# Column blocks in pairs, two of eight K-tile pairs as seven products of sums, feed-forward in three parts

## The chip, the cores and the metric

The kernel runs on one core of one Trainium2 chip. The metric is device microseconds (us) of one execution, lower is better. A measured time is the median of several executions.

## The reference, cut to what matters

The reference is a two-layer decoder trunk on x of 256 tokens by 2048, all in float32. Layer 0 mixes with a gated unit and sparse attention between two projections, layer 1 with a short convolution between two projections; each layer ends in a feed-forward, and a norm closes the trunk.

```python
def swiglu(h, w_gate, w_up, w_down):
    return (jax.nn.silu(h @ w_gate) * (h @ w_up)) @ w_down      # 2048 -> 5632 -> 2048
...
for i in range(DEPTH):
    hn = rmsnorm(h, norm_mix[i])
    mix = sgu_nsa_mixer(hn, w_in_ab[j], w_out_ab[j], ...) if i % 2 == 0 else short_conv_mixer(hn, w_in_c[j], conv_w[j], w_out_c[j])
    h = h + mix
    h = h + swiglu(rmsnorm(h, norm_ffn[i]), w_gate[i], w_up[i], w_down[i])
return rmsnorm(h, norm_f)
```

## The kernel before, in words

Tokens are two tiles of 128 (m = 0, 1). Every projection is a product of activations (stationary, 128 x 128 tiles) and weights (moving, 128 rows by 512 columns, NW). Both are kept as a sum of two float32r parts, high and low, and a product is three matmuls into one PSUM bank: xh*wh, xh*wl, xl*wh (L99, L100, L101 in `Stream.multiply`).

`Stream` holds the whole order of the work. `gemm` (L44) lays down the units of one column block of 512: a unit is two K tiles, for both m, so 2 x 2 x 3 = 12 matmuls; 2048 rows of weights are 8 units. A block uses two PSUM banks of the pool `pg` (four banks), so blocks alternate. Weights come by SP's queue in loads of 1 MB (two units) into three raw buffers (`load`, L67). `split` (L75) makes a unit's parts: ACT copies the raw tile to `wh` (L82), DVE subtracts it from the raw tile to give `wl` (L83), both 1024 wide. There are four buffers of parts, so splits run three units ahead of PE (`ahead`, L103): the split for unit i+3 is issued behind unit i's matmuls and waits for the buffer of unit i-1. `run` (L111) goes through the units: matmuls, splits ahead, the block's `done` if it was its last unit, then the hooks that were laid on this unit (`at`, `after`). Each engine has its instructions in this order and takes them in order.

In the feed-forward (L746) gate and up blocks alternate, 11 of each per layer; `done_gate_ff` (L760) applies silu on ACT out of PSUM, `done_up` multiplies on DVE out of PSUM (L769), and one unit later eight PE transposes (L227) bring the product to K-major form, which ACT and DVE split (L238, L239). All 44 K tiles of it are kept, and the down projection runs as four column blocks over 44 K tiles, 22 units each. `norm_from` (L268) adds a block's two banks to h (L276), sums squares on ACT (L250), and transposes h for the next operand. The convolution (L792 to L848) has 12 input blocks (cg, z, bg for each of four) and four output blocks. `last` (L865) ends the kernel: the last four units run m by m, so that the first half is normed and stored while the second is multiplied.

At the start SP issues row0, x's first piece (256 tokens by 256 columns), the first raw load, x's second piece, the second raw load, x's third piece, the third raw load; ACT issues the other five pieces of x. The first four raw loads are 512 KB. PE transposes the first two pieces before the first unit.

Of the kernel before, what the change touches and what calls it, by code (L numbers as in the profile page):

```python
# [27 lines left out]
NEG = -1e30  # L28
AHEAD = 3
PROBS, VALUES = 4, 6  # L30


class Stream:


    def __init__(self, nc, raws, parts, psg):
        self.nc, self.raws, self.parts, self.psg = nc, raws, parts, psg
        self.raw_plan, self.units = [], []
        self.raw, self.hl = {}, {}
        self.loaded = self.split_to = 0  # L40
        self.hooks = {}
        self.at_unit = 0

    def gemm(self, w, groups, n0, src, done, tail=0, between=None):  # L44
# [3 lines left out]
        for gi, g in enumerate(groups):  # L48
            k0, gk = g if isinstance(g, tuple) else (g, 4)
            ri = len(self.raw_plan)  # L50
            self.raw_plan.append((w[k0 * P:(k0 + gk) * P, n0:n0 + NW].rearrange("(k p) n -> p k n", p=P), gk * NW))
            for j in range(gk // 2):
                self.units.append({
                    "raw": ri, "j": j, "k0": k0 + 2 * j, "src": src, "chunk": chunk, "free": j == gk // 2 - 1,
                    "first": gi == 0 and j == 0, "last": gi == len(groups) - 1 and j == gk // 2 - 1, "tail": 0,
                })
            if between and gi < len(groups) - 1:
                ap, use = between.pop(0)
                self.units.append({"raw": len(self.raw_plan), "j": 0, "use": use, "free": True})
                self.raw_plan.append((ap, 2 * NW))  # L60
        if tail:
            self.units[-tail]["tail"] = tail

# [3 lines left out]
    def load(self):  # L67
        if self.loaded < len(self.raw_plan):
            ap, n = self.raw_plan[self.loaded]
            t = self.raws.tile([P, 4 * NW], F32, name="raw")  # L70
            self.nc.sync.dma_start(out=t[:, :n].rearrange("p (k n) -> p k n", n=ap.shape[-1]), in_=ap)
            self.raw[self.loaded] = t.rearrange("p (k n) -> p k n", n=NW)
            self.loaded += 1

    def split(self, pieces=(slice(0, 2),)):  # L75
        u = self.units[self.split_to]
        nc = self.nc
        src = self.raw[u["raw"]][:, 2 * u["j"]:2 * u["j"] + 2, :]
        hv = self.parts.tile([P, 2, NW], F32R, name="wh")
        lv = self.parts.tile([P, 2, NW], F32R, name="wl")  # L80
        for ks in pieces:
# [889 lines left out]
```

## Time and profile before

| | us |
|---|---|
| median of three runs | 2187.59 (2186.87 to 2188.07) |
| the profiled execution | 2187.05 |
| its span, first to last instruction | 2185.3 |
| PE busy | 2174.6, 9900 matmuls |
| DVE busy | 1149.6, 1269 instructions |
| ACT busy | 988.3, 1178 instructions |

The span is what the trace covers; the rest of the execution's time lies around it. Busy is the time in which an engine has an instruction running, PE's ends being modelled. In a row of a group, "x767" is a count, the figure before the comma its busy us, the one behind it the mean ns of one instruction.

### The profile page before, as it was taken

The numbers are of one execution on the slowest core, as the hardware profiler recorded it, in microseconds if no ns is written. First come the engines' busy times: TensorE is split into PE (matmuls) and PEld (weight loads), VectorE is DVE, ScalarE is ACT, GpSimd is POOL, SyncE is SP. The second block draws the span as 40 slices with busy tenths as digits, with TensorE's granted clock in tenths as the row PEclk, the third lists the DMA queues.
The fourth block names the chain that finished last, engine by engine and source line by source line (L and its number), as shares of the span: only waits on it lengthen the run. The fifth ranks groups of instructions, "written<-read, shape, count | busy, mean of one in ns | idle before, by whom it ended". The sixth has DMA issues, their size and how long they took to land.

```text
span 2185.3 us, 24414 instructions
## 1 busy us (share of the span) xinstructions
PE 2174.6 (100%) x9900; PEld 1796.8 (82%) x9900; DVE 1149.6 (53%) x1269; ACT 988.3 (45%) x1178; POOL 28.3 (1%) x59
## 2 busy tenths in 40 slices
PE   9999999999999999999999999999999999999998
PEld 7887788888888888888888888888888888888886
DVE  6577655555444544544455555554554455444444
ACT  6456545444444444444444444444444444444443
POOL 2000000000000000000000000000000000000000
PEclk9999999999999999999999999999999999999999
DMA  7664455665555555555556555556555555556553
GB/s 261 204 198 134 136 176 190 193 193 183 188 190 191 192 191 188 188 187 190 192 184 201 185 182 191 190 187 192 192 193 191 188 186 186 192 193 197 197 193 135
DMA packets 214577, 410.95 MB, mean 188 GB/s; under 512 B 6744, under 2 KB 18448, under 8 KB 214464
## 3 DMA queue, kind: packets, MB, share of 16 engines
q1 hardware_dynamic: 210416, 404.52, 56.9%
q10 hardware_dynamic: 3664, 3.63, 0.5%
q8 instruction: 77, 1.26, 0.2%
q0 software_dynamic: 384, 1.25, 0.2%
q14 instruction: 36, 0.29, 0.0%
HBM read 407.27 MB, written 2.10 MB: 187 GB/s over the span
## 4 chain that ended last, share of the span: by engine, by line
PE 99%; issue 0%; DMA 0%; DVE 0%; SPq 0%; POOLq 0%; POOL 0%; ACT 0%; DVEq 0%
PE pg L99 32%; PE pg L101 32%; PE pg L100 32%; PE pm L227 2%; PE pm L537 0%; PE pm L614 0%; PE pm L403 0%; PE pm L570 0%; DMA h<-in_x_dram 0%; PE pm L501 0%; PE pm L688 0%; PE pm L617 0%; PE pm L577 0%; POOLq L966 0%; POOL nf_r L899 0%
## 5 line engine op out<-in xcount | busy, mean ns | idle before, releaser
L83 DVE TENSOR_TENSOR wl<-raw,wh 128x1024 fp32r<-128x1024 f32 (+1 forms) x769 | 939.1, 1224 | 923.0 <-ACT wh L82 920.4
L82 ACT ACTIVATE wh<-raw 128x1024 fp32r<-128x1024 f32 (+1 forms) x769 | 812.0, 1059 | 962.3 <-PE pg L101 952.7
L99 PE MATMUL pg<-wh,a_h 128*128 128x512 f32 x2080 | 820.6, 394 | 0.0
L101 PE MATMUL pg<-wh,a_l 128*128 128x512 f32 x2080 | 810.6, 390 | 0.0
L100 PE MATMUL pg<-wl,a_h 128*128 128x512 f32 x2080 | 810.0, 389 | 0.0
L101 PEld LDWEIGHTS pg<-wh,a_l 128*128 128x128 f32 x2080 | 390.7, 188 | 82.1
L100 PEld LDWEIGHTS pg<-wl,a_h 128*128 128x128 f32 x2080 | 391.0, 188 | 81.7 <-issue 2.2
L99 PEld LDWEIGHTS pg<-wh,a_h 128*128 128x128 f32 x2080 | 390.9, 188 | 81.4 <-issue 2.1
L99 PE MATMUL pg<-wh,t_h 128*128 128x512 f32 x704 | 274.3, 390 | 0.0
L101 PE MATMUL pg<-wh,t_l 128*128 128x512 f32 x704 | 273.9, 389 | 0.0
L100 PE MATMUL pg<-wl,t_h 128*128 128x512 f32 x704 | 273.9, 389 | 0.0
L101 PEld LDWEIGHTS pg<-wh,t_l 128*128 128x128 f32 x704 | 132.1, 188 | 27.4
L100 PEld LDWEIGHTS pg<-wl,t_h 128*128 128x128 f32 x704 | 132.2, 188 | 27.3
L99 PEld LDWEIGHTS pg<-wh,t_h 128*128 128x128 f32 x704 | 132.2, 188 | 27.3
L99 PE MATMUL pg<-wh,y 128*128 128x512 f32 x128 | 50.4, 394 | 0.0
L99 PE MATMUL pg<-wh,z_h 128*128 128x512 f32 x128 | 50.2, 392 | 0.0
L101 PE MATMUL pg<-wh,y 128*128 128x512 f32 x128 | 49.9, 390 | 0.0
L101 PE MATMUL pg<-wh,z_l 128*128 128x512 f32 x128 | 49.9, 390 | 0.0
L100 PE MATMUL pg<-wl,y 128*128 128x512 f32 x128 | 49.8, 389 | 0.0
L100 PE MATMUL pg<-wl,z_h 128*128 128x512 f32 x128 | 49.8, 389 | 0.0
L239 DVE TENSOR_TENSOR t_l<-pm,t_h 128x512 fp32r<-128x512 f32 x44 | 28.4, 686 | 32.4 <-ACT t_h L238 32.4
L238 ACT ACTIVATE t_h<-pm 128x512 fp32r<-128x512 f32 x44 | 23.9, 595 | 46.2 <-PE pm L227 46.2
(182 smaller groups left out, 780.3 us busy)
## 6 DMA issues: line engine op xcount, KB each, us to landing
raw<-in_w_gate_dram SPq DMA_DIRECT2D x88, 1024.0 KB, 5.2
raw<-in_w_up_dram SPq DMA_DIRECT2D x88, 1024.0 KB, 5.2
raw<-in_w_down_dram SPq DMA_DIRECT2D x88, 1024.0 KB, 5.1
raw<-in_w_in_c_dram SPq DMA_DIRECT2D x48, 1024.0 KB, 5.1
raw<-in_w_in_ab_dram SPq DMA_DIRECT2D x34, 1024.0 KB, 5.2
raw<-in_w_out_ab_dram SPq DMA_DIRECT2D x16, 1024.0 KB, 5.1
raw<-in_w_out_c_dram SPq DMA_DIRECT2D x16, 1024.0 KB, 5.1
raw<-in_w_in_ab_dram SPq DMA_DIRECT2D x4, 512.0 KB, 6.7
```

The costliest lines, as they stand in the source:

```text
L82: nc.scalar.activation(hv[:, ks], src[:, ks], AF.Copy)
L83: nc.vector.tensor_sub(lv[:, ks], src[:, ks], hv[:, ks].bitcast(F32))
L99: nc.tensor.matmul(ps[m], xh[:, kt, sl], hv[:, k, :], start=u["first"] and k == 0, stop=False)
L100: nc.tensor.matmul(ps[m], xh[:, kt, sl], lv[:, k, :], start=False, stop=False)
L101: nc.tensor.matmul(ps[m], xl[:, kt, sl], hv[:, k, :], start=False, stop=u["last"] and k == 1)
L227: nc.tensor.transpose(t[:, k * S + m * P:k * S + (m + 1) * P], src[:, m, c + k * P:c + (k + 1) * P], ident)
L238: nc.scalar.activation(dh[:, k0:k0 + 2, :], t, AF.Copy)
L239: nc.vector.tensor_sub(dl[:, k0:k0 + 2, :], t, dh[:, k0:k0 + 2, :].bitcast(F32))
```

## The change

Stages from the first feed-forward on run as blocks of two column blocks (`Stream.block`), n = 0 and 1, over eight pairs of K tiles. A block uses four `pg` banks, one for each n and m (`BANK`). Pairs of K tiles 0 to 3, 5 and 7 are multiplied as before: two units ("n" in the pattern) of 12 matmuls. Pairs 4 and 6 (`SUMS`) go as seven products instead of eight: four units ("s") with 2, 2, 2 and 1 products of three matmuls, some of sums of weights and some of sums of activations. Four of the seven products gather over both pairs in banks P1, P5, P6, P7 of the other pool, which transposes also use; the rest add to the block's own banks. The sums of weights are four DVE additions, 512 wide, ahead of the first "s" unit's split (`sums13`); `sum2` overwrites half of a raw tile. An "s" unit's split is 1024 wide, the fourth's 512. The sums of activations are made when the operand is split (`x_split`): three DVE subtractions and a second split, one unit later.

Behind the unit of the last P5 and P7 products, `summed` puts the four banks together in two SBUF tiles g and u: a copy on ACT, four DVE instructions. When the block ends, `done` adds the block's own banks: n = 0 behind the last unit, n = 1 behind the first unit of the next block. Gate and up are now the two column blocks of one block; silu and product run on SBUF tiles, and their transposes come in two fours at the end of the next block's units 2 and 3. In down and output blocks `add_to_h` adds g and u to h and then the banks to h.

The feed-forward runs in three parts of 4, 4 and 3 gate/up blocks (`PARTS`), each followed by the down product over its own K tiles, two blocks each, added to h. Blocks over 12 K tiles have the order N6 with one pair of seven products. F8 is N8 with the sums one unit later; it is used where an operand is new: each layer's first gate/up block, the first convolution block, the first output block. The last two column blocks of layer 1's last part stay single, as the tail was.

Raw loads are all 512 KB, in six buffers, and eight from the first output block of layer 0 on (`widen`), where the buffers of parts become five, so splits run four units ahead. At the start two raw loads are issued where one was.

```diff
+RAWS = 6
+MORE = 2
...
+PARTS = (4, 4, 3)
+SUMS = {4: 0, 6: 1}
+BANK = ((1, 3), (2, 7))
+P1, P5, P6, P7 = FREE = (0, 4, 5, 6)
...
+    def widen(self, pool):
+        self.ring.insert(self.slot, (pool, len(self.ring)))
+        self.sums = pool
+        self.free += [pool] * MORE
...
+    def block(self, ws, form, src, begun, summed, done):
...
+        for kp, seven in order:
+            k0 = 2 * kp
+            wk = [w[(kb + k0) * P:(kb + k0 + 2) * P, n0:n0 + NW].rearrange("(k p) n -> p k n", p=P) for w, kb, n0 in ws]
+            def t(k, m, k0=k0):
+                return lambda: src.tile(k0 + k, m)
+            def s(i, kp=kp):
+                return lambda: src.sum(kp, i)
+            if not seven:
+                for n in range(2):
+                    queue["n"].append((wk[n], {"frees": 1, "mms": [(k, t(k, m), BANK[n][m]) for m in range(MT)
+                                                                    for k in range(2)]}))
+            else:
+                queue["s"].append((wk, t, s))
+                queue["s"].extend([None] * 3)
...
+                def sums13(ra=ra, rb=rb, ts=ts, sum2=sum2, sum4=sum4):
+                    a, b = self.raw[ra], self.raw[rb]
+                    ts.append(self.sums.tile([P, 3, NW], F32, name="ts", bufs=2))
+                    self.nc.vector.tensor_add(ts[0][:, 0], a[:, 0], b[:, 0])
+                    self.nc.vector.tensor_add(ts[0][:, 1], b[:, 0], b[:, 1])
+                    sum2()
+                    sum4()
...
+                sevens = [
+                    {"raw": ra, "prep": sums13, "frees": 1, "mms": [(0, t(0, 0), P1), (1, t(1, 0), BANK[0][0])]},
+                    {"raw": rb, "frees": 1, "mms": [(0, s(2), P6), (1, s(3), BANK[1][0])]},
+                    {"raw": rb, "ts": ts, "at": 0, "mms": [(0, s(1), P5), (1, s(0), P7)]},
+                    {"raw": rb, "ts": ts, "at": 2, "w": 1, "mms": [(0, t(1, 1), BANK[0][1])]},
+                ]
+                u = sevens.pop(0)
+            else:
+                u = sevens.pop(0)
...
+        self.on(last_sum, lambda: summed(0, chunk["banks"]))
+        self.on(last_sum + 1, lambda: summed(1, chunk["banks"]))
+        end = len(self.units)
+        self.soon[end - 1] = lambda: done(0, chunk["banks"])
+        self.soon[end] = lambda: done(1, chunk["banks"])
+        for u, fn in begun:
+            self.on(first + u, fn)
+    def on(self, unit, fn, *args):
+        self.hooks.setdefault(unit, []).append(lambda: fn(*args))
     def at(self, delay, fn):
         self.hooks.setdefault(self.at_unit + delay, []).append(fn)
...
+        while self.free and self.loaded < len(self.raw_plan):
+            ap = self.raw_plan[self.loaded]
+            pool = self.free.pop(0)
+            t = pool.tile([P, 2 * NW], F32, name="raw", bufs=RAWS if pool is self.raws else MORE)
+            v = t.rearrange("p (k n) -> p k n", n=NW)
+            self.nc.sync.dma_start(out=t.rearrange("p (k n) -> p k n", n=ap.shape[-1]), in_=ap)
+            self.raw[self.loaded] = v
+            self.home[self.loaded] = pool
...
+    def split(self, pieces=None):
+        i = self.split_to
+        u = self.units[i]
...
+            u["prep"]()
+        w = u.get("w", 2)
+        src = u["ts"][0][:, u["at"]:u["at"] + w] if "ts" in u else self.raw[u["raw"]]
+        pool, k = self.ring[self.slot]
+        self.slot = (self.slot + 1) % len(self.ring)
+        hv = pool.tile([P, 2, NW], F32R, name=f"wh{k}")
+        lv = pool.tile([P, 2, NW], F32R, name=f"wl{k}")
+        for ks in pieces or (slice(0, w),):
             nc.scalar.activation(hv[:, ks], src[:, ks], AF.Copy)
+            if "then" in u:
+                u["then"]()
...
-        self.hl[self.split_to] = (hv, lv)
...
+            self.free.append(self.home[u["raw"]])
+        self.load()
...
+        while self.split_to < min(len(self.units), i + 1 + min(len(self.ring) - 1, 2 + i // 8)):
...
+            if i in self.soon:
+                self.soon[i]()
...
+    def x_split(src, dst, kp, gain=None):
+        ks = slice(2 * kp, 2 * kp + 2)
+        if kp not in SUMS:
+            split_T([src.rearrange("p (k m) c -> p k (m c)", k=2)], (dst.h, dst.l), 2 * kp, gain)
+            return
...
+        v = a.rearrange("p (k m) c -> p k (m c)", k=2)
+        nc.vector.tensor_sub(xs[:, 4:6], a[:, 0:2], a[:, 1:4:2])
+        nc.vector.tensor_sub(xs[:, 6], a[:, 0], xs[:, 5])
+        nc.vector.tensor_sub(xs[:, 7], a[:, 2], xs[:, 6])
+        def parts():
+            i = SUMS[kp]
+            nc.scalar.activation(dst.h[:, ks], v, AF.Copy)
+            nc.scalar.activation(dst.sh[:, i], xs[:, 4:], AF.Copy)
+            nc.vector.tensor_sub(dst.l[:, ks], v, dst.h[:, ks].bitcast(F32))
+            nc.vector.tensor_sub(dst.sl[:, i], xs[:, 4:], dst.sh[:, i].bitcast(F32))
+        st.at(1, parts)
+    def x_pair(src, c, dst, kp, gain=None):
+        t = transposed_bank(src, c).rearrange("p k (m c) -> p (k m) c", m=MT)
+        st.at(1, lambda: x_split(t, dst, kp, gain))
...
+    def summed(part, b):
+        if part == 0:
+            g, u = (late["pool"].tile([P, MT, NW], F32, name=n) for n in ("ga", "ub"))
+            late["g"], late["u"] = g, u
+            nc.scalar.activation(g[:, 0], b[P1], AF.Copy)
+            return
+        g, u = late["g"], late["u"]
+        nc.vector.tensor_sub(u[:, 0], b[P6], g[:, 0])
+        nc.vector.tensor_sub(g[:, 1], b[P7], u[:, 0])
+        nc.vector.tensor_sub(u[:, 1], b[P5], g[:, 1])
+        nc.vector.tensor_add(u[:, 0], b[P5], u[:, 0])
...
+    def add_to_h(n2, squares=None):
+        c0 = 2 * n2 * NW
+        def sums(part, b):
+            summed(part, b)
+            if part:
+                for n, t in enumerate((late["g"], late["u"])):
+                    hs = h[:, :, c0 + n * NW:c0 + (n + 1) * NW]
+                    nc.vector.tensor_add(hs, hs, t)
+        def done(n, b):
+            for m in range(MT):
+                hs = h[:, m, c0 + n * NW:c0 + (n + 1) * NW]
+                nc.vector.tensor_add(hs, b[BANK[n][m]], hs)
+            if squares:
+                st.at(1, lambda: [squares(2 * n2 + n, m) for m in range(MT)])
+        return sums, done
     stage = ExitStack()
...
+    N8 = [(k, k in SUMS) for k in range(8)], "nnnnn sns sns sns sns nnn"
+    F8 = [(k, k in (4, 6)) for k in range(8)], "nnnnnn sns sns sns sns nn"
+    N6 = [(k, k in SUMS) for k in range(6)], "nnn nn sn sn sn s nn"
...
+    def feed_forward(layer, rname, norm):
+        c0 = 0
+        for part, nb in enumerate(PARTS):
+            for c in range(c0, c0 + nb):
+                def done(n, b, c=c, kb=4 * c0):
+                    g, u = late["g"], late["u"]
+                    for m in range(MT):
+                        t = (g, u)[n][:, m]
+                        nc.vector.tensor_add(t, b[BANK[n][m]], t)
+                    def later():
+                        for m in range(MT):
+                            r = R[rname][:, m:m + 1]
+                            if n == 0:
...
+                            else:
+                                nc.vector.scalar_tensor_tensor(g[:, m], u[:, m], r, g[:, m], op0=ALU.mult, op1=ALU.mult)
+                    st.at(1, later)
+                def pairs(b, c=c, c0=c0):
+                    if c == c0 and b == 0:
+                        second_operand()
+                    x_pair(late["g"], b * S, src_x, 2 * (c - c0) + b)
+                st.block([(w_gate[layer], 0, c * NW), (w_up[layer], 0, c * NW)], F8 if c == 0 else N8, src_a, begun[:],
+                         summed, done)
+                begun[:] = [(2, lambda p=pairs: p(0)), (3, lambda p=pairs: p(1))]
+            last = part == len(PARTS) - 1
+            for n2 in range(2):
+                if last and layer == 1 and n2 == 1:
+                    break
+                sums, done = add_to_h(n2, norm[0] if last else None)
+                ws = [(w_down[layer], 4 * c0, 2 * n2 * NW), (w_down[layer], 4 * c0, (2 * n2 + 1) * NW)]
+                st.block(ws, N8 if nb == 4 else N6, src_x, begun[:], sums, done)
+                begun[:] = norm[1](n2) if last else []
+            c0 += nb
...
+    squares, pair, scale = norm_from("c1", g_mix[1])
+    feed_forward(0, "f0", (squares, then_pairs(pair, scale)))
...
+        def gated(n, b):
+            if c == 0 and n == 0 and b == 0:
+                second_operand()
+            y = cv[c + n][:, 2 * b:2 * b + 2]
+            t = transposed_bank((late["g"], late["u"])[n], b * S)
+            def later():
+                nc.vector.tensor_mul(y, t, y)
+                st.at(1, lambda: x_split(y.rearrange("p k (m c) -> p (k m) c", m=MT), src_x, 2 * (c + n) + b))
+            st.at(1, later)
+        if c == 0:
+            return done, [(2, lambda: gated(0, 0)), (2, lambda: gated(0, 1)), (3, lambda: gated(1, 0)),
+                          (3, lambda: gated(1, 1))]
+        return done, [(2, lambda: gated(0, 0)), (3, lambda: gated(0, 1)), (4, lambda: gated(1, 0)),
...
+    order = F8
+    for c in (0, 2):
+        for cc in (c, c + 1):
+            done, then = done_cz(cc)
+            st.block([(wc, 0, D + cc * NW), (wc, 0, 2 * D + cc * NW)], order, src_a, begun[:], summed, done)
+            begun[:] = then
+            order = N8
+        done, then = done_bg(c)
+        st.block([(wc, 0, c * NW), (wc, 0, (c + 1) * NW)], N8, src_a, begun[:], summed, done)
+        begun[:] = then
+    squares, pair, scale = norm_from("f1", g_ffn[1])
+    begin = then_pairs(pair, scale)
+    for n2 in range(2):
+        sums, done = add_to_h(n2, squares)
+        st.block([(w_out_c[0], 0, 2 * n2 * NW), (w_out_c[0], 0, (2 * n2 + 1) * NW)], N8 if n2 else F8, src_x, begun[:], sums,
+                 done)
+        begun[:] = begin(n2)
...
+    u0 = len(st.units)
+    for c in (2, 3):
+        w = w_down[1][4 * sum(PARTS[:2]) * P:]
+        st.gemm(w, [0, 4, 8], c * NW, src_x, last(c), tail=AHEAD + 1 if c == 3 else 0)
...
+    free = st.free
     for b in range(3):
+        st.free = free[:2]
         st.load()
         if b < 2:
             x_load(nc.sync, b + 1)
```

## Rows read from the trace of the kernel before

**Rows 1.** Page: busy time, granted clock by slice, shares of the chain

```profile
PE 2174.6 (100%) x9900; PEld 1796.8 (82%) x9900; DVE 1149.6 (53%) x1269; ACT 988.3 (45%) x1178; POOL 28.3 (1%) x59
...
PEclk9999999999999999999999999999999999999999
...
PE 99%; issue 0%; DMA 0%; DVE 0%; SPq 0%; POOLq 0%; POOL 0%; ACT 0%; DVEq 0%
PE pg L99 32%; PE pg L101 32%; PE pg L100 32%; PE pm L227 2%; PE pm L537 0%; PE pm L614 0%; PE pm L403 0%; PE pm L570 0%; DMA h<-in_x_dram 0%; PE pm L501 0%; PE pm L688 0%; PE pm L617 0%; PE pm L577 0%; POOLq L966 0%; POOL nf_r L899 0%
```

**Rows 2.** Stretch of feed-forward 0: us, engines' busy us, clock, DMA share, GB/s

```profile
403.00:805.00 402.00, 402.00 (x1816) 333.65 (x1815) 200.64 (x182) 173.57 (x182) 0.00 (x0) 1.00 0.59 189
```

**Rows 3.** Timeline of ACT, five gate units: start us, us, instruction, idle before

```profile
632.46 1.06 ACT L82 ACTIVATE wh<-raw 128x1024 fp32r<-128x1024 f32 x1 [1.66 <-PE pg L101]
...
643.34 1.06 ACT L82 ACTIVATE wh<-raw 128x1024 fp32r<-128x1024 f32 x1 [1.66 <-PE pg L101]
```

**Rows 4.** Page, costliest groups: first matmul of each triple, by operand

```profile
L99 PE MATMUL pg<-wh,a_h 128*128 128x512 f32 x2080 | 820.6, 394 | 0.0
...
L99 PE MATMUL pg<-wh,t_h 128*128 128x512 f32 x704 | 274.3, 390 | 0.0
...
L99 PE MATMUL pg<-wh,y 128*128 128x512 f32 x128 | 50.4, 394 | 0.0
L99 PE MATMUL pg<-wh,z_h 128*128 128x512 f32 x128 | 50.2, 392 | 0.0
```

**Rows 5.** Waits of engines and SP's queue: total us, times, longest

```profile
ACT wh L82 <- PE pg L101: 952.7, 600, 3.1
DVE wl L83 <- ACT wh L82: 920.4, 670, 3.3
...
ACT wh L82 <- DMA raw<-in_w_in_ab_dram: 2.3, 2, 2.0
...
SPq L71 <- DVE wl L83: 1925.7, 380, 11.8
```

**Rows 6.** Groups of DVE by shape: count, busy us, mean ns, idle

```profile
L83 DVE TENSOR_TENSOR wl<-raw,wh 128x1024 fp32r<-128x1024 f32 x767 | 937.6, 1225 | 923.0 <-ACT wh L82 920.4
...
L540 DVE SCALAR_TENSOR_TENSOR s<-dist,pm 128x256 f32<-128x256 f32 x16 | 6.0, 418 | 4.2 <-PE pm L537 4.1
...
L877 DVE TENSOR_TENSOR h<-h,nfg 128x1024 f32<-128x1024 f32 x3 | 3.7, 1218 | 0.0
...
L901 DVE TENSOR_TENSOR h<-h,nfg 128x512 f32<-128x512 f32 x2 | 1.4, 689 | 0.0
```

**Rows 7.** Groups of ACT by shape, columns the same

```profile
L82 ACT ACTIVATE wh<-raw 128x1024 fp32r<-128x1024 f32 x767 | 810.9, 1060 | 962.3 <-PE pg L101 952.7 <-ACT wh L82 3.7 <-DMA raw<-in_w_in_ab_dram 2.3
...
L238 ACT ACTIVATE t_h<-pm 128x512 fp32r<-128x512 f32 x44 | 23.9, 595 | 46.2 <-PE pm L227 46.2
```

**Rows 8.** Timeline of DVE: instructions close behind each other, some merged

```profile
121.16 2.36 DVE L83 TENSOR_TENSOR wl<-raw,wh 128x1024 fp32r<-128x1024 f32 x2 [1.84 <-ACT wh L82]
...
138.19 0.19 DVE L419 TENSOR_TENSOR hq<-hw 128x30 f32<-128x30 f32 x1
138.41 0.18 DVE L420 TENSOR_SCALAR hq<-hq 128x30 f32<-128x30 f32 x1
...
627.20 1.29 DVE L239 TENSOR_TENSOR t_l<-pm,t_h 128x512 fp32r<-128x512 f32 x2 [1.47 <-ACT t_h L238]
```

**Rows 9.** Timeline of PE at the start: x's second piece, first matmuls

```profile
6.78 1.12 PE L227 MATMUL pm<-ident,h 128*128 128x128 f32 x4 [0.31 <-DMA h<-in_x_dram]
...
8.65 0.63 PE L101 MATMUL pg<-wh,a_l 128*128 128x512 f32 x1
9.08 0.63 PE L99 MATMUL pg<-wh,a_h 128*128 128x512 f32 x1
```

**Rows 10.** Stretches at the start, columns as in rows 2

```profile
3.00:7.00 4.00, 3.42 (x15) 2.61 (x14) 0.64 (x3) 1.34 (x4) 3.44 (x16) 1.00 0.99 312
7.00:10.00 3.00, 3.00 (x10) 2.38 (x10) 2.21 (x6) 1.82 (x5) 2.59 (x10) 1.00 1.06 391
```

More of the change, by code (lines that the diff above doesn't have):

```diff
@@ L49, in gemm @@
             k0, gk = g if isinstance(g, tuple) else (g, 4)
[L50 to L56, printed above, removed]
+            for k in range(k0, k0 + gk, 2):
+                ri = self.plan(w[k * P:(k + 2) * P, n0:n0 + NW].rearrange("(k p) n -> p k n", p=P))
+                self.units.append({"raw": ri, "k0": k, "src": src, "chunk": chunk, "frees": 1, "first": gi == 0 and k == k0,
+                                   "last": gi == len(groups) - 1 and k == k0 + gk - 2, "tail": 0})
@@ L91, in multiply @@
         u = self.units[i]
-        ps = u["chunk"]["ps"]
         hv, lv = self.hl[i]
-        xh, xl = u["src"]
+        c = u["chunk"]
+        if "mms" in u:
+            for x, (j, op, key) in enumerate(u["mms"]):
+                uses = c["uses"][key]
+                if uses[0] == (i, x):
+                    c["banks"][key] = self.bank(key)
+                ps = c["banks"][key]
+                xh, xl = op()
+                nc.tensor.matmul(ps, xh, hv[:, j, :], start=uses[0] == (i, x), stop=False)
+                nc.tensor.matmul(ps, xh, lv[:, j, :], start=False, stop=False)
+                nc.tensor.matmul(ps, xl, hv[:, j, :], start=False, stop=uses[-1] == (i, x))
+            return
+        ps = c["ps"]
         for k in range(2):
@@ L849, in done_bg @@
+            for m in range(MT):
+                hs = h[:, m, c * NW:(c + 1) * NW]
+                nc.vector.tensor_add(hs, ps[m], hs)
+                squares(c, m)
+            st.at(1, lambda: pair(2 * c))
+            st.at(1 if c < 3 else 2, lambda: pair(2 * c + 1))
+            if c == 3:
+                st.at(3, scale)
         return done
     for c in range(4):
-        st.gemm(wc, G4, D + c * NW, src_a, done_cg(c))
-        st.gemm(wc, G4, 2 * D + c * NW, src_a, done_z(c))
-        st.gemm(wc, G4, c * NW, src_a, done_bg(c))
@@ new lines, in open_conv, with done_cz, done, conv @@
+    def open_conv():
+        cv["p"] = top.enter_context(tc.tile_pool(name="convt", bufs=2, reuse_waits="tile"))
+        r2 = cv["r2"] = const.tile([P, MT], F32, name="r2")
+        nc.vector.tensor_mul(r2, R["c1"], R["c1"])
+    def done_cz(c):
+        def done(n, b):
+            if c == 0 and n == 0:
+                open_conv()
+            g, u = late["g"], late["u"]
+            for m in range(MT):
+                t = (g, u)[n][:, m]
+                nc.vector.tensor_add(t, b[BANK[n][m]], t)
+            def later():
+                if n:
+                    nc.vector.tensor_mul(g, u, g)
+                else:
+                    for m in range(MT):
+                        nc.scalar.activation(g[:, m], g[:, m], AF.Copy, scale=cv["r2"][:, m:m + 1])
+            st.at(1, later)
+        def conv(b):
+            if b == 0:
+                cv[c] = cv["p"].tile([P, 4, S], F32, name="zc")
+            v = transposed_bank(late["g"], b * S)
+            def later():
+                for k in range(2):
+                    kt = 4 * c + 2 * b + k
+                    o, z = cv[c][:, 2 * b + k], v[:, k]
+                    nc.scalar.activation(o, z, AF.Copy, scale=g_conv[2][:, kt:kt + 1])
+                    for j, lag in ((1, 1), (0, 2)):
+                        nc.vector.scalar_tensor_tensor(o[:, lag:], z[:, :S - lag], g_conv[j][:, kt:kt + 1],
+                                                       o[:, lag:], op0=ALU.mult, op1=ALU.add)
+            st.at(1, later)
+        return done, [(2, lambda: conv(0)), (3, lambda: conv(1))]
```

321 lines of the change are left out of this document (160 added, 161 removed).

## The prediction

> **What bounds the kernel now.** I read the page first. PE is busy for the whole span, the granted clock is full in every slice, and the chain that ended last is 99% PE, nearly all of it the three matmuls of the split product; DVE is busy 53% and ACT 45% [rows 1]. A table by stretch says the same of the feed-forward alone: PE 402.0 of 402.0 us, DVE 200.6, ACT 173.6, DMA 0.59 [rows 2]. So in the stages that change, time is the number of matmuls times their pace. The pace is read from ACT's copies, which follow PE's units of 12 matmuls: from 632.46 to 643.34 us there are four steps, so 2.72 us a unit and 0.2267 us a matmul [rows 3]. (The rows' 390 ns is a latency; the matmuls overlap.) The page's groups count 2080+704+128+128 = 3040 such triples, 9120 matmuls [rows 4], or 2067 us.
>
> Nobody feeds PE late: ACT waits 952.7 us for PE to give back a buffer of parts, DVE waits 920.4 us for ACT, and SP's loads wait 1925.7 us for DVE to be done with a raw buffer [rows 5]. All three walk in step behind PE.
>
> The profiled execution took 2187.05 us around a span of 2185.3; the median of the runs is 2187.59, 0.54 more. The sum is made against 2187.05.
>
> **The change, part by part.**
>
> *Fewer matmuls.* A pair of K tiles with a pair of column blocks needs 2x2x2 = 8 products of three matmuls; as seven it needs 21 matmuls in place of 24. I count the pairs in the code. Gate/up: 11 blocks in each of two layers, two pairs each: 44. Down: four N8 blocks a layer (16 pairs in all), two N6 blocks in layer 0 and one in layer 1 (3 pairs); the last two column blocks of layer 1 stay plain. Convolution: 6 input blocks and 2 output blocks, 16 pairs. That is 79 pairs, 237 matmuls, 237 x 0.2267 = **53.7 us** less. Shapes and the number of transposes stay. PE has no wait to win back, so nothing is gained beyond this.
>
> *More vector work.* Per pair, instead of two splits of 1024 wide (1.225 us) there are three and one of 512, and four sums of 512 (0.69 us between SBUF tiles) [rows 6]: 1.92 + 2.76 = 4.7 us, over 79 pairs 369 us. The 41 blocks each assemble four PSUM results, 4 x 0.69 (113 us). Then: two adds of 1024 into h for 13 down/output blocks (1.22 each, 32 us), PSUM adds of gate/up (61), down (22) and convolution (16), and the sums of the activations for 18 operand pairs at about 1.7 us (30; priced by the 256-wide row of 0.42). DVE goes from 1150 to about 1793 us, some 84% of the new span. A gate/up block costs DVE 12 x 1.225 + 2 x (3 x 1.225 + 0.69) + 18 x 0.69 + 2 x 0.69 = 37.2 us against PE's 186 x 0.2267 + 0.9 = 43.1; a down block 36.9 against 42.2. ACT: 1.69 us more a pair (1.06 a full copy, 0.6 a half) [rows 7] and 48 us of copies: about 1170 us, 55%. Both fit beside PE on average.
>
> *The order.* DVE takes its queue in order, so I walk it where a deadline stands. Independent instructions come closer than their length: two of 686 ns in 1.29 us and two of 1225 in 2.36, a pace of 0.60 and 1.13; an instruction that needs the one before starts 0.03 us after its end (0.19 long, 0.22 apart) [rows 8]. ACT's copy puts a split's start 1.09 us after PE returned the buffer.
>
> The first deadline is the accumulator banks. A block uses all four, and the next block's first unit starts with the bank that the first add of `done` must have read. In a gate/up block DVE has, from the end of the last unit of sums, 11.56 us of PE time (units of 2.72, 0.68 and 3 x 2.72): split and assembly until 5.3, three splits until 8.6, and the add only waits for PE: no loss. A down or output block in N8 order adds 2 x 1.13 for h: 1.42 + 1.13 + 2.64 (assembly) + 2.26 + 3 x 1.13 + 0.69 = 11.53 against 11.56, no margin; I take 0.2 us for each of nine, 1.8 (ends 0 and 1.0 each). In N6, and in the one F8 output block, only two units lie behind the sums: 8.84 us of PE time against 1.42 + 1.13 + 2.64 + 2.26 + 2 x 1.13 + 0.69 = 10.4: PE waits 1.6 us, four times, **6.4 us** (ends 0 and 2.4 each).
>
> The second is PE's transposes of gate x up at the end of unit 2. Before them DVE has `done(1)`, a split, the four sums for the first unit of sums, a split and the product: ready 7.4 us after the block's start, needed at 8.16. Margin 0.7, no loss taken (end 0.5 for 22 blocks). After the convolution's gating, `parts` for the pair of tiles 4 comes one unit before its use behind five other instructions: 0.6 us, once.
>
> *Start.* x's second piece now stands behind two raw loads instead of one, 512 KB more. PE starts its transposes when that piece lands (6.78 us) [rows 9], with the DMA engines saturated: 312 GB/s from 3 to 7 us, 391 from 7 to 10 [rows 10], so it comes 1.3 to 1.7 us later. The third piece stands behind 1 MB more, about 3 us, and has a unit of time. I take +1.5, ends 0 and 3 (that piece late as well). The 2.3 us that ACT waited for early raw loads [rows 5] were not on PE's path. Loads are halved in size and doubled in number; six, then eight, buffers of 512 KB keep more in flight than three of 1 MB, and the DMA share rises as the time shrinks, 0.59 to about 0.61. Cost nothing; were the cover gone, PE would wait for raw tiles. SP only issues loads.
>
> *Feed-forward in three parts, the end.* The down products keep their count; only the h adds above are new. The end (add, squares, scale, store) is as before: nothing.
>
> Sum: -53.7 + 1.5 + 6.4 + 1.8 + 0.6 = -43.4; 2187.05 - 43.4 = 2143.65, and with the 0.54 of the runs **2144.2 us**.
>
> **Rivals.**
>
> *Full drain.* If DVE's independent instructions don't overlap in these chains, each costs its length plus 0.03. Then the N8 down deadline is missed by 0.95 us (nine times), N6 and F8 by 2.4 (four), the transposes by 0.15 (22), with start and gating as above: 8.6 + 9.6 + 3.3 + 2.1 = 23.6, about 2157 us. The Trainium skill states just that ("VectorE: DVE Perf Modes", section "The DRAIN you can't avoid"): the next instruction does not issue until the pipeline is empty, and chaining without semaphores gains nothing. The paces of 0.60 and 1.13 in [rows 8] disagree with it for plain sequences; the new chains have more dependences.
>
> *DVE falls behind in the stretches of sums.* The four sums (2.6 us) precede the split of the first unit of sums in a queue that also carries the splits for the next 2.72 us unit. If buffer returns and ACT's copies do not line up, each pair costs PE 0.4 us: 79 x 0.4 = 32 us more, about 2176. Against it: four units of lookahead, some 8 us.
>
> *Slower.* PE's waits at the bank handover cost it its pace. At the start, where PE has had gaps, matmuls come 0.43 us apart (8.65 and 9.08) [rows 9], close to what the lower of the two clock levels, 1.2 GHz, would give, though the granted clock of that stretch is written as 1.00 [rows 10]; later, with PE never idle, they come 0.2267 apart. If a handover waits and the next unit of 12 runs at that pace, it costs 12 x 0.2 = 2.4 us beside a wait of 1.6; at all 41 blocks 164 us, about 2298. It decides for "slower" from 54/41 = 1.3 us a block. The Trainium skill ("TensorE: Matmul & The Clock Gate", section "A second HAM failure mode: psum-queue depth-cycling") describes a clock that falls and rises where PE idles briefly between groups of matmuls as banks are cycled; no row here shows it, as PE does not wait.
>
> That the saving itself is not made is hardly possible: the instruction count fixes it.
>
> **How the numbers follow.** A measurement of this kernel tells about 0.2% (4.4 us) from no change, so faster means under 2183. Forecast with its own bounds, 2136 to 2153: 0.66. Everything hidden, 2133 to 2136: 0.05. Full drain, 2153 to 2166: 0.12. DVE behind: 0.09, of which 0.02 ends within 0.2%. Slower by the clock or by a stall of this size at every block: 0.08. Range 2133 to 2166 (0.83). Faster 0.90, same 0.02, slower 0.08.
>
> **What would show it.** PE's count 9900 less 237, PE busy near 100% outside the start, clock full in every slice; DVE near 84%, ACT near 55%; small PE waits for the `h` adds at the ends of N6 blocks and none elsewhere; x's second piece landing near 8.3 us. It would be wrong if PE shows waits for splits (`wl`) inside blocks, if DVE's pace in the sums is over 0.72 us, if the clock falls in any slice, or if SP's loads are waited for.

## The result, and the profile after

The changed kernel took 2151.99 us (median of 4 runs, 2151.69 to 2152.04) beside 2187.38 for the kernel before on the same chip: ratio 0.9838, 95% interval 0.9821 to 0.9855. That is 35.4 us less. Forecast were 43.4 less and 2144.2 us; the time lies in the range, the direction is right, and 7.8 us of cost were not in the sum. The profiled execution's span is 2149.6 us, 35.7 below the 2185.3 of before.

From the page of the changed kernel: busy time by engine, granted clock by slice, and the chain by engine and line.

```profile
PE 2128.9 (99%) x9663; PEld 1750.0 (81%) x9663; DVE 1709.6 (80%) x2139; ACT 1145.3 (53%) x1411; POOL 24.1 (1%) x59
...
PEclk9999999999999999999999999999999999999999
...
PE 93%; DVE 3%; issue 2%; ACT 1%; DMA 0%; SPq 0%; POOLq 0%; POOL 0%; DVEq 0%; ACTq 0%
```

Beside [rows 1]: PE has exactly 237 instructions less, it is still the bound, and the clock is full in every slice. DVE has gone from 53% to 80%. The chain now has 7% outside PE.

The waits of PE in the changed kernel: what waited for what, total us, times, longest.

```profile
PE pg L230 <- DVE h L509: 4.8, 3, 1.6
PE pm L371 <- DMA h<-in_x_dram: 1.8, 1, 1.8
PE pg L239 <- DVE h L509: 1.6, 1, 1.6
...
PE pg L240 <- DVE wl L211: 0.8, 1, 0.8
PE pg L239 <- ACT wh L208: 0.7, 1, 0.7
```

The first and third lines are the handover of the accumulator banks, four times. The other lines shown are the first 17 us. No unit inside a block of sevens waits for the split of its weights.

DVE's groups by shape in the changed kernel: count, busy us, mean ns, idle before.

```profile
L211 DVE TENSOR_TENSOR wl<-raw,wh 128x1024 fp32r<-128x1024 f32 x767 | 924.4, 1221 | 253.8 <-ACT wh L208 245.1
...
L138 DVE TENSOR_TENSOR ts<-raw 128x512 f32<-128x512 f32 x79 | 54.7, 692 | 2.7
...
L474 DVE TENSOR_TENSOR ga<-pm,ub 128x512 f32<-128x512 f32 x41 | 28.4, 692 | 4.3
...
L504 DVE TENSOR_TENSOR h<-h,ub 128x1024 f32<-128x1024 f32 x13 | 15.8, 1218 | 0.0
```

Each price is within 4 ns of the one read from [rows 6]. The counts 79, 41 and 13 are those of the forecast.

**The handover as it came.** DVE's timeline at the end of the first N6 block: start us, us, instruction, idle before.

```profile
1030.99 1.23 DVE L211 TENSOR_TENSOR wl<-raw,wh 128x1024 fp32r<-128x1024 f32 x1 [0.21 <-ACT wh L208]
1032.14 0.68 DVE L473 TENSOR_TENSOR ub<-pm,ga 128x512 f32<-128x512 f32 x1
...
1034.86 1.22 DVE L504 TENSOR_TENSOR h<-h,ga 128x1024 f32<-128x1024 f32 x1
1035.99 1.22 DVE L504 TENSOR_TENSOR h<-h,ub 128x1024 f32<-128x1024 f32 x1
1037.12 2.35 DVE L211 TENSOR_TENSOR wl<-raw,wh 128x1024 fp32r<-128x1024 f32 x2
1039.39 1.28 DVE L509 TENSOR_TENSOR h<-pg,h 128x512 f32<-128x512 f32 x2
```

PE's timeline at the same place, and the stretch around it (us, busy us of PE, PEld, DVE, ACT, POOL, clock, DMA share, GB/s).

```profile
1038.24 0.39 PE L232 MATMUL pg<-wh,y 128*128 128x512 f32 x1
1040.22 0.47 PE L230 MATMUL pg<-wh,y 128*128 128x512 f32 x1 [1.60 <-DVE h L509]
```

```profile
1040.00:1044.00 4.00, 3.77 (x17) 3.17 (x18) 4.00 (x6) 2.22 (x5) 0.00 (x0) 1.00 0.93 288
```

The walk of the prediction can be laid beside it: assembly 2.72 us (1032.14 to 1034.86; forecast 2.64), the `h` adds 2.26 (forecast 2.26), two splits 2.27 (forecast 2.26), then the adds that free the bank. PE's next matmul starts 1.98 us after the last one instead of 0.23, so 1.75 us lost, where 1.6 were forecast. The next matmuls come at full pace and the clock is written 1.00.

**The start as it came.** PE and then ACT in the changed kernel.

```profile
8.46 1.11 PE L371 MATMUL pm<-ident,h 128*128 128x128 f32 x4 [1.83 <-DMA h<-in_x_dram]
...
13.98 0.60 PE L371 MATMUL pm<-ident,h 128*128 128x128 f32 x4
15.27 0.51 PE L239 MATMUL pg<-wh,a_h 128*128 128x512 f32 x1 [0.69 <-ACT wh L208]
16.53 0.50 PE L240 MATMUL pg<-wl,a_h 128*128 128x512 f32 x1 [0.76 <-DVE wl L211]
...
295.39 1.04 PE L371 MATMUL pm<-ident,h 128*128 128x128 f32 x8
```

```profile
7.40 5.98 ACTq L320 DMA_DIRECT2D h<-in_x_dram  x4
...
9.88 0.37 ACTq L320 DMA_DIRECT2D h<-in_x_dram  x1
...
13.43 0.84 ACT L387 ACTIVATE a_h<-pm,gains 128x256 fp32r<-128x256 f32 x2 [5.74 <-DMA h<-in_x_dram]
```

x's second piece is transposed at 8.46 us, 1.68 later than in [rows 9]; forecast was 1.3 to 1.7. But the loss grows. PE's second unit stands behind a gap at 15.27, and the last row, the first transposes of the first feed-forward's norm, came earlier in the kernel before:

```profile
291.33 1.04 PE L227 MATMUL pm<-ident,h 128*128 128x128 f32 x8
```

So **4.1 us** are lost, not 1.5. ACT's rows say why, as a first reading: from 7.40 to 13.38 its queue issues four loads of x's later pieces, and its next computation, the parts of x's second piece, starts at 13.43, though PE had transposed that piece soon after 8.46.

The row of 5.98 us is four issues in one line. Each takes 0.37 or 0.38 us (the row at 9.88 is one of them, from a narrower window). They start at 7.40, 9.88, 11.52 and 13.01, each 0.02 us behind the landing of an earlier load (7.38, 9.86, 11.50, 12.99), and the trace records for each a wait for that load's completion semaphore. In this stretch the program's loads share eight such semaphores, and a load is not issued before the last load with its semaphore has landed. The chain that ended last, in order of time (start us, us, what), has the fourth issue, which waited for x's third piece:

```profile
4.67 8.31 DMA h<-in_x_dram
12.99 0.02 issue
13.01 0.37 ACTq L320
```

In the kernel before, ACT's issues of x met loads that had landed, the latest at 8.28 us, and the last three took 1.58 us together.

### The profile page after: what moved, and what is told of

It is laid out like the page before. It is cut to its first block, busy times and chain, and to the rows that moved or that the text cites. A ratio compares the mean times of both kernels' runs of the same rounds, so it can differ in the third digit from the quotient of the medians.

```text
span 2149.6 us, 26495 instructions
## 1 busy us (share of the span) xinstructions
PE 2128.9 (99%) x9663; PEld 1750.0 (81%) x9663; DVE 1709.6 (80%) x2139; ACT 1145.3 (53%) x1411; POOL 24.1 (1%) x59
## 4 chain that ended last, share of the span: by engine, by line
PE 93%; DVE 3%; issue 2%; ACT 1%; DMA 0%; SPq 0%; POOLq 0%; POOL 0%; DVEq 0%; ACTq 0%
PE pg L230 22%; PE pg L232 22%; PE pg L231 22%; PE pg L239 5%; PE pg L241 5%; PE pg L240 5%; PE pm L232 3%; PE pm L231 3%; PE pm L230 3%; PE pm L371 2%; DVE wl L211 2%; ACT wh L208 1%; PE pm L758 0%; PE pm L835 0%; DMA h<-in_x_dram 0%
## 5 line engine op out<-in xcount | busy, mean ns | idle before, releaser
L230 PE MATMUL pg<-wh,a_h 128*128 128x512 f32 x1456 | 572.1, 393 | 1.7 <-DVE h L509 1.6
L232 PE MATMUL pg<-wh,a_l 128*128 128x512 f32 x1456 | 567.4, 390 | 0.0
L231 PE MATMUL pg<-wl,a_h 128*128 128x512 f32 x1456 | 566.7, 389 | 0.0
L230 PEld LDWEIGHTS pg<-wh,a_h 128*128 128x128 f32 x1456 | 273.4, 188 | 59.1 <-issue 2.0
L230 PE MATMUL pg<-wh,y 128*128 128x512 f32 x646 | 253.7, 393 | 3.2 <-DVE h L509 3.2
L232 PE MATMUL pg<-wh,y 128*128 128x512 f32 x646 | 251.7, 390 | 0.0
L231 PE MATMUL pg<-wl,y 128*128 128x512 f32 x646 | 251.5, 389 | 0.0
L211 DVE TENSOR_TENSOR wl<-ts,wh 128x1024 fp32r<-128x1024 f32 (+1 forms) x158 | 150.9, 955 | 99.4 <-ACT wh L208 99.1
L208 ACT ACTIVATE wh<-ts 128x1024 fp32r<-128x1024 f32 (+1 forms) x158 | 133.7, 846 | 136.5 <-PE pg L232 136.5
L230 PEld LDWEIGHTS pg<-wh,y 128*128 128x128 f32 x646 | 121.3, 188 | 30.0 <-ACT wh L208 4.0
L232 PEld LDWEIGHTS pg<-wh,y 128*128 128x128 f32 x646 | 121.2, 188 | 25.6
L231 PEld LDWEIGHTS pg<-wl,y 128*128 128x128 f32 x646 | 121.3, 188 | 24.5
L239 PE MATMUL pg<-wh,a_h 128*128 128x512 f32 x288 | 120.8, 419 | 0.7 <-ACT wh L208 0.7
L240 PE MATMUL pg<-wl,a_h 128*128 128x512 f32 x288 | 113.0, 393 | 0.8 <-DVE wl L211 0.8
L241 PE MATMUL pg<-wh,a_l 128*128 128x512 f32 x288 | 113.4, 394 | 0.0
L239 PE MATMUL pg<-wh,y 128*128 128x512 f32 x176 | 69.1, 393 | 1.6 <-DVE h L509 1.6
L241 PE MATMUL pg<-wh,y 128*128 128x512 f32 x176 | 68.5, 389 | 0.0
L240 PE MATMUL pg<-wl,y 128*128 128x512 f32 x176 | 68.5, 389 | 0.0
```

The source lines that it names most:

```text
L208: nc.scalar.activation(hv[:, ks], src[:, ks], AF.Copy)
L211: nc.vector.tensor_sub(lv[:, ks], src[:, ks], hv[:, ks].bitcast(F32))
L230: nc.tensor.matmul(ps, xh, hv[:, j, :], start=uses[0] == (i, x), stop=False)
L231: nc.tensor.matmul(ps, xh, lv[:, j, :], start=False, stop=False)
L232: nc.tensor.matmul(ps, xl, hv[:, j, :], start=False, stop=uses[-1] == (i, x))
L239: nc.tensor.matmul(ps[m], xh, hv[:, k, :], start=u["first"] and k == 0, stop=False)
```

## The experiments

**1. The start: is it x's place in the queue?** Two edits thin out the raw loads ahead of x. The first leaves one load before each piece:

```diff
     for b in range(3):
-        st.free = free[:2]
+        st.free = free[:1]
         st.load()
         if b < 2:
             x_load(nc.sync, b + 1)
+    st.free = free[3:]
+    st.load()
```

> At the start one raw load stands before each piece of x, as in the kernel before; the other three raw loads are issued right behind them, so as many bytes are outstanding when ACT issues its five pieces. Theory (queue on ACT): the start costs 4.1 us, of which 1.7 is x's second piece landing late (8.46 against 6.78) and the rest is ACT, whose splits stand behind its own issues of x, which take 5.98 us for four because so much is outstanding: then the second piece lands at 6.8 again, ACT's issues stay slow, and 1.5 to 2.5 us are won, about 2150. Rival (order of bytes alone): all 4.1 are won, 2148.

2153.25 us (2151.35 to 2153.56), ratio 0.9843 (0.983 to 0.9857): 1.3 above the changed kernel, so neither expectation held. PE's timeline and a stretch of it:

```profile
7.25 1.12 PE L371 MATMUL pm<-ident,h 128*128 128x128 f32 x4 [0.62 <-DMA h<-in_x_dram]
...
15.48 0.50 PE L239 MATMUL pg<-wh,a_h 128*128 128x512 f32 x1 [2.95 <-ACT wh L208]
```

```profile
14.00:20.00 6.00, 3.76 (x10) 2.74 (x11) 5.25 (x7) 4.66 (x9) 0.00 (x0) 0.77 1.07 374
```

The piece is there 1.2 us sooner and nothing is won: PE's second unit waits for ACT until 15.48, and in the stretch behind that wait the granted clock is 0.77 (matmuls 0.43 us apart until 20.4). ACT's queue issues its four loads from 7.22 for 6.37 us, again each 0.02 us behind the landing of an earlier load, the last at 13.20.

The second edit was to keep only three raw loads outstanding:

```diff
-        st.free = free[:2]
+        st.free = free[:1]
...
+    on(2, st.free.extend, free[3:])
```

> As the kernel before at the start: three raw loads, and the other three buffers are first used behind unit 2. Both theories: all of the 4.1 us are won, about 2148; ACT's five issues take 2.6 us again. If less than 3 us are won, the start's cost is something else.

2153.92 us (2153.43 to 2154.49), ratio 0.9848 (0.9835 to 0.9862). It did not limit what it was meant to limit: the loads that follow the first splits took the fresh buffers at once, so SP issued five loads in a row from 3.74 us, and ACT's queue held four issues for 6.46 us from 6.92. It missed its 2148, says nothing on its own theory and repeats the reading of the first.

**2. The start: is it ACT's issues?** SP issues x's pieces 4 to 8 behind its raw loads; ACT issues none.

```diff
             x_load(nc.sync, b + 1)
+    for c in range(3, 8):
+        x_load(nc.sync, c)
...
-    for c in range(3, 8):
-        x_load(nc.scalar, c)
```

> The five later pieces of x are issued by SP behind the six raw loads; ACT issues nothing at the start. The first pieces keep the changed kernel's order. Theory (ACT held by its own issues): x's second piece still lands near 8.5 us, but ACT's next work no longer waits until 13.4 us, and the second unit of matmuls starts near 14.4 in place of 15.3 to 16.5: 2 to 3 us less than 2152, about 2149.5. Rival (too many bytes ahead of x): the later pieces now stand behind all 3 MB and land late, nothing is won or up to 3 us are lost.

2148.72 us (2148.63 to 2148.85), ratio 0.9824 (0.981 to 0.9837): 3.3 less. ACT's and PE's timelines:

```profile
9.36 0.84 ACT L387 ACTIVATE a_h<-pm,gains 128x256 fp32r<-128x256 f32 x2 [2.05 <-PE pm L371]
```

```profile
8.30 1.02 PE L371 MATMUL pm<-ident,h 128*128 128x128 f32 x4 [2.47 <-DMA h<-in_x_dram]
...
13.51 0.48 PE L239 MATMUL pg<-wh,a_h 128*128 128x512 f32 x1
...
292.60 1.04 PE L371 MATMUL pm<-ident,h 128*128 128x128 f32 x8
```

With x's piece as late as before (8.30), ACT starts its parts at 9.36 instead of 13.43, PE's second unit follows without a gap, and 295.39 becomes 292.60. What is left against 291.33 is 1.3 us: the late piece alone, which the forecast had at 1.5. So the later pieces' issues on ACT cost the other 2.8: 2.0 of it in the second unit (13.98 to 19.17 us from its transposes to the next in the changed kernel, 13.15 to 16.35 here), 0.6 in the pace of the first (4.76 us against 4.17), and the rest in the piece's landing. Why the first unit reaches its full pace sooner here is not shown. SP's five issues wait for landings too (7.60 behind 7.59, 9.71 behind 9.69, 11.14 behind 11.12), but no computation stands behind them.

The start varies: of the five variants of experiments 3, 5 and 6 that leave it as it is, four have these transposes at 295.27 to 295.87 us and one at 297.50. The medians' 3.3 is the firmer figure.

**3. The handover.** The assembled results are added into `h` behind the adds that free the banks, not ahead of them.

```diff
         def sums(part, b):
             summed(part, b)
-            if part:
-                for n, t in enumerate((late["g"], late["u"])):
-                    hs = h[:, :, c0 + n * NW:c0 + (n + 1) * NW]
-                    nc.vector.tensor_add(hs, hs, t)
...
                 nc.vector.tensor_add(hs, b[BANK[n][m]], hs)
+            hs = h[:, :, c0 + n * NW:c0 + (n + 1) * NW]
+            nc.vector.tensor_add(hs, hs, (late["g"], late["u"])[n])
```

> The adds of g and u into h move from in front of the bank adds to behind them; as much work. Theory (handover of the banks): PE's waits of 1.75 us at the ends of three N6 blocks and the F8 output block and of 0.17 us at nine others go, 8.5 us less, about 2143.5. Rival (DVE's total is the bound): the waits turn up elsewhere, and less than 3 us are won.

2143.03 us (2142.64 to 2143.34), ratio 0.9798 (0.9785 to 0.9812): 9.0 less, 8.5 expected. The only row left of PE's waits for a bank:

```profile
PE pg L230 <- DVE h L505: 0.6, 3, 0.2
```

**4. Both together.** First with the start edit that did not work:

> The three-load start and the later adds into h together. Theory: the two add up, 12.6 us less, about 2139.4, with PE busy near its span but for the start and the tail. Rival: DVE's total binds after one is mended, and the second brings less than half of its own.

2145.27 us (2144.03 to 2145.7), ratio 0.9807 (0.9793 to 0.982): missed by 5.9, and 2.2 worse than the handover's mend alone, as that start edit is 1.9 worse than none. The handover's mend took 8.65 off that start too, so the rival did not come. Then with SP issuing raw loads and x's pieces in turn, none on ACT, and the handover's mend of 3:

```diff
-    for b in range(3):
-        st.free = free[:2]
+    for b in range(6):
+        st.free = free[:1]
         st.load()
-        if b < 2:
-            x_load(nc.sync, b + 1)
+        x_load(nc.sync, b + 1)
+    x_load(nc.sync, 7)
...
-    for c in range(3, 8):
-        x_load(nc.scalar, c)
```

> SP issues raw loads and pieces of x in turn, one each, ACT issues nothing at the start, and g and u are added to h behind the banks. Theory: the start's 4.1 us and the handover's 9 us are both won, about 2139. Rival: the start's cost lies in the bytes outstanding and only the 9 us are won, 2143.

**2138.35 us** (2138.21 to 2138.95), ratio 0.9777 (0.9763 to 0.979): 13.6 less than the changed kernel and faster than both. Its longest wait of PE is 1.4 us, ahead of the first transposes. Its page:

```profile
PE 2124.7 (99%) x9663; PEld 1749.8 (82%) x9663; DVE 1711.7 (80%) x2139; ACT 1145.0 (54%) x1411; POOL 25.7 (1%) x59
```

**5. The pairing without the sevens.** All eight products of every pair, no sums; blocks, column pairs, three parts and start as in the changed kernel. The vectors that held the assembled results are copied from the banks.

```diff
-        if kp not in SUMS:
+        if True:
...
-    N8 = [(k, k in SUMS) for k in range(8)], "nnnnn sns sns sns sns nnn"
-    F8 = [(k, k in (4, 6)) for k in range(8)], "nnnnnn sns sns sns sns nn"
-    N6 = [(k, k in SUMS) for k in range(6)], "nnn nn sn sn sn s nn"
+    N8 = F8 = [(k, False) for k in range(8)], "n" * 16
+    N6 = [(k, False) for k in range(6)], "n" * 12
...
-                        nc.vector.tensor_add(t, b[BANK[n][m]], t)
+                        nc.vector.tensor_copy(t, b[BANK[n][m]])
```

> No pair is made of sums: all pairs take eight products in plain units, and g and u are copied from the banks instead of being assembled. Blocks of two columns, the three parts of the feed-forward and the start stay as in the changed kernel. Theory: PE's 53.7 us come back and the 9 us of waits at the ends of blocks go, about 2197, so that pairing and parts alone cost some 9 us against the kernel before, 4 of them at the start. Rival (the sums cost PE waits inside blocks too): the difference to 2152 is under 40 us.

2193.61 us (2193.21 to 2196.28), ratio 1.0032 (1.002 to 1.0044). From its page:

```profile
PE 2176.7 (99%) x9900; PEld 1795.3 (82%) x9900; DVE 1231.0 (56%) x1409; ACT 987.6 (45%) x1178; POOL 23.9 (1%) x59
```

The rest of the change alone makes the kernel 6.5 us slower than before in the same runs, and the profiled execution 5.8: 4.1 of it the start (its 295.39 is the changed kernel's) and 1.9 the transposes. Behind 285 us the kernel before has 42 groups of eight transposes; here, as in the changed kernel, there are 9 groups of eight and 66 of four. From the last matmul ahead of a group to the twelfth behind it, PE takes 0.91 us more than twelve paces of 0.2267 for a group of eight, and 0.48 for a group of four: 38.2 us in all before, 40.1 here.

About 2197 was expected. The sevens take off 41.6, little more than the 40 of the rival that has the sums cost waits inside blocks too: 53.7 less the handover and the small terms of the table below.

**6. How much room has DVE?** One sum of each pair is written once, twice or four times more (repeated work):

```diff
                     self.nc.vector.tensor_add(ts[0][:, 1], b[:, 0], b[:, 1])
+                    for _ in range(1):
+                        self.nc.vector.tensor_add(ts[0][:, 1], b[:, 0], b[:, 1])
```

> The second sum of every pair is written twice, one instruction of 0.69 us more on DVE in each of 79 pairs (repeated work, nothing left out). Theory (DVE has a margin of about half a microsecond before PE's transposes of gate x up, and none at the bank handover): the transposes stay in time or are late by 0.1 us in 22 blocks, each of the 13 down and output blocks waits about 0.6 us more: 2152 + 8 + 2 = about 2162 us, no granted clock below full. Rival (DVE at 80% has room everywhere): within 2 us of 2152.

2158.52 us (2158.23 to 2158.81), ratio 0.9867 (0.9852 to 0.9881). 6.5 us, of the theory's 10, and not where it put most of them: the four waits at the handover are 1.6 us as before, while the period of a gate/up block grows from 43.13 us (transposes at 498.59 and 541.72) to 43.33 (499.64 and 542.97). 22 times 0.2 is 4.4 of the 6.5. Measured as in 5, all groups of transposes together hold PE 6.8 us longer than in the changed kernel (the profiled execution is 6.9 longer behind the start), so the rest stands at other transposes.

> The same with two instructions more in each pair. Theory: transposes of gate x up late by 0.7 us in 22 blocks (15 us), the bank handover later by 1.2 us in 13 blocks (16 us): about 2183 us, the clock still full, since PE's waits of up to 1.75 us at the bank handover left it full in the changed kernel and only waits of about 2 us in front of transposes were followed by a lower one with four more sums. Rival (any wait over about 1 us in front of the transposes costs the next dozen matmuls their pace): 22 x 2 us more, about 2225 us.

2178.49 us (2177.8 to 2179.77), ratio 0.9957 (0.994 to 0.9974): 26.5 us. PE's waits and its timeline at one gate/up block:

```profile
PE pm L373 <- DVE ga L1003: 12.6, 44, 1.0
PE pg L232 <- DVE h L511: 4.8, 3, 1.6
```

```profile
503.38 0.33 PE L373 MATMUL pm<-ident,ga 128*128 128x128 f32 x1 [0.16 <-DVE ga L1003]
504.04 0.55 PE L373 MATMUL pm<-ident,ga 128*128 128x128 f32 x3 [0.33 <-DVE ga L1003]
504.34 0.47 PE L232 MATMUL pg<-wh,a_h 128*128 128x512 f32 x1
```

The period is 44.05 us (503.38 to 547.42), 0.92 more, 22 times or 20 us (25.5 over all groups of transposes); the clock of the stretch from 504 to 509 us is 1.00. So the transposes of gate x up are the nearest deadline, and the second sum is paid there nearly in full; the handover does not move at all, since the sums stand ahead of the point from which its 8.84 us count. My expectations of 8 and 16 us there were both wrong.

> One of the four sums of weights of each pair is made five times: four DVE adds of 512 more, 2.9 us a pair, 227 us in all, DVE's total then some 90% of the span. Theory (deadlines in DVE's queue): the margin of 0.7 us ahead of PE's transposes at unit 2 is overdrawn by 2.2 us in some 25 blocks (gate/up and the convolution's), 50 to 60 us more, about 2207. Rival (only the total counts, and it still fits beside PE): within 10 us of 2152.

2247.83 us (2245.0 to 2253.36), ratio 1.028 (1.0266 to 1.0294): 96 us, where 50 to 60 were expected. PE's waits, its timeline and a stretch of the same block:

```profile
PE pm L373 <- DVE ga L1003: 44.6, 44, 2.5
```

```profile
507.07 0.33 PE L373 MATMUL pm<-ident,ga 128*128 128x128 f32 x1 [1.61 <-DVE ga L1003]
507.73 0.55 PE L373 MATMUL pm<-ident,ga 128*128 128x128 f32 x3 [0.33 <-DVE ga L1003]
...
508.99 0.63 PE L232 MATMUL pg<-wh,a_h 128*128 128x512 f32 x1
509.42 0.63 PE L233 MATMUL pg<-wl,a_h 128*128 128x512 f32 x1
```

```profile
507.00:512.00 5.00, 4.60 (x15) 3.54 (x16) 3.87 (x7) 0.60 (x1) 0.00 (x0) 0.66 0.76 218
```

Behind PE's waits at the transposes the granted clock is now 0.66 over this stretch (0.50, the lower of its two levels, from 509 to 512 us), and matmuls come 0.43 us apart. That is what the rival "slower" described, at another place and at two thirds of its price: eight matmuls at 0.2 more are 1.6 us here, where it had 2.4.

## Why the prediction was right, and where its sizes were off

| term | forecast | shown by | measured |
|---|---|---|---|
| 237 matmuls | -53.7 | count 9663; eight products against sevens | 237 fewer; -41.6 net of the costs below |
| start | +1.5 | transposes at 295.39 against 291.33 | +4.1 |
| banks, N6 and F8 | +6.4 | four starts 1.75 us late | +7.0 |
| banks, N8 | +1.8 | nine starts 0.17 us late | +1.5 |
| gating, pair 4 | +0.6 | PE's starts at 1355 us, not tested | +0.4 |
| transposes in fours | 0 | experiment 5 | +1.9 |
| second matmul behind a handover | 0 | 0.31 us behind the first in place of 0.23, 13 times | +1.0 |
| other short delays of PE | 0 | five, of 0.27 to 0.40 us, not tested | +1.6 |
| not placed | 0 | what remains of -35.7 | about +0.5 |

*Fewer matmuls.* Right in count, and that PE gains nothing beyond them was right too.

*The order.* Right in place and size: the handover is late at just the four blocks named, 1.75 us instead of 1.6, and moving the `h` adds gave back 9.0 us. The terms of 6.4 and 1.8 were the ones with the most working behind them, and a walk along DVE's queue with the paces of [rows 8] did what it was meant to. No large errors hid each other: only the N8 banks and pair 4 cost less than forecast, 0.5 us together.

*Start.* This is the term that was mis-sized: +1.5 against 4.1. x's second piece by itself cost 1.3 us, near the forecast. The step that failed is what the term left out: five loads of x that ACT's queue issues stand ahead of its next computations, and the prediction does not speak of them, so they stood at nothing without a reason. It looked for more loss in the third piece, which "has a unit of time". That piece landed at 12.99 us, 4.0 later than before (9.02), and PE transposed it at 13.98 without a wait; but its landing let ACT's last issue go. "Cost nothing", said of the loads in flight, failed with it: ACT's issues met semaphores of loads that landed as late as 12.99 us, and ACT computed nothing from 7.69 to 13.43.

*The transposes.* Margin 0.7 us and no loss forecast; no loss by waiting came in the gate/up block below. DVE's timeline and then PE's in it:

```profile
492.86 0.69 DVE L143 TENSOR_TENSOR ts<-raw 128x512 f32<-128x512 f32 x1
493.46 0.68 DVE L144 TENSOR_TENSOR ts<-raw 128x512 f32<-128x512 f32 x1
494.18 0.69 DVE L135 TENSOR_TENSOR raw<-ts,raw 128x512 f32<-128x512 f32 x1
...
496.65 1.41 DVE L1001 SCALAR_TENSOR_TENSOR ga<-ub,r_f,ga 128x512 f32<-128x512 f32 x2
```

```profile
498.59 0.60 PE L371 MATMUL pm<-ident,ga 128*128 128x128 f32 x4
```

DVE's two products end at 498.06 us and PE's transposes start at 498.59, so the margin was 0.53, and one dependent sum more (0.72 us) overruns it by the 0.2 us measured. "Shapes and the number of transposes stay" is right, but 33 of the groups of eight became 66 groups of four, 1.9 us that the sum had at nothing.

*More vector work.* 1793 us were forecast and the page has 1709.6, but the prices are not at fault. The lengths of all of DVE's instructions add up to 1179 us in the kernel before and 1814 in the changed one: 635 added, where the terms gave 643. The page counts time in which two instructions overlap once, and the forecast had added whole lengths to its 1150. Nothing in the time hung on it.

*Not in the sum.* Five us had no term. PE's starts place all but some 0.5 of them: the transposes in fours, the second matmul behind each of the 13 late handovers, and five short delays of PE (at 412, 1128 and 1480 us inside groups of transposes, at 1020 and 2088 us at a matmul with the low part of the activations). What ends these five delays no run tested.

*The rivals.* "Full drain" (2157 us) lies closer to the time than it deserves. By it, sums that don't depend on each other would start 0.71 us apart; in the rows above they start 0.60 apart (492.86 and 493.46), and those that depend 0.72 (493.46 and 494.18). The Trainium skill's rule ("VectorE: DVE Perf Modes", "The DRAIN you can't avoid") is not borne out by these rows as the prediction took it; the same section says that a next instruction which is not held back starts earlier, and with that the rows agree. "DVE falls behind" did not happen: no wait of PE for a split inside a block of sevens. "Slower" did not happen in the changed kernel either: behind 1.60 us at the handover the clock stayed at 1.00. The Trainium skill's picture of a clock that falls and rises as PE idles between groups of matmuls while banks are cycled ("TensorE: Matmul & The Clock Gate", "A second HAM failure mode: psum-queue depth-cycling") is not what these handovers of banks show; a clock that falls behind short waits shows with four more sums, in front of transposes, 0.66 of the full clock in the stretch behind 1.61 and 0.33 us of waiting.

## What to carry to other kernels

When work moves from the bound engine to one with room, what counts is not that engine's busy share but each deadline in its queue: DVE at 80% had 0.5 us of room at one of them and was 1.75 us late at another. Put what no one waits for (here adds into `h`) behind what frees a buffer. When a change sets more or earlier loads in flight, look at who else issues loads then: an engine that issues DMAs between its computations holds its computations up with them, and an issue can itself wait for an earlier load to land.

## What the hardware showed that was not expected

An issue of a load was short in every row, and still held an engine for 6 us. On ACT's queue one takes 0.37 to 0.49 us in the kernel before and in the changed one. Four took 5.98 us in the changed kernel (6.37 and 6.46 in the two start variants) because each waited for the semaphore of a load that had not landed. Those loads were slow to land: issued between 2.2 and 4.7 us, they landed between 7.4 and 13.0, with the DMA engines' share above 1.0 (1.08 from 10 to 14 us). When SP issued the five itself, they took 5.13 us, and no wait of PE stands behind them.

The clock after a wait is not told by the wait's length alone: it stayed at 1.00 behind 1.60 us at the bank handover, and behind 0.69 and 0.76 us at the start, and was 0.66 behind 1.61 and 0.33 us around transposes, 0.77 behind 2.95 us at the start. Nor do the written clock and the pace always agree: in the changed kernel matmuls start 0.43 us apart from 9.80 to 13.21 us, and the stretch from 10 to 14 us is written 1.00.
